# One DMA transpose per attention weight tile instead of two to four, a fourth running-product buffer, and the carries on VectorE

## The chip, the cores and the metric

The kernel runs on one NeuronCore of a Trainium2 chip. The metric is the time of one execution on the device, in microseconds (us). The median over several runs is what is compared.

The core has five engines that each work through their own list of instructions in order: TensorE (PE, with its weight loads PEld), VectorE (DVE), ScalarE (ACT), GpSimd (POOL) and SyncE (SP), which here issues nearly all DMA transfers. Waits between engines go by semaphores. The order on each engine was fixed when the program was built.

## The reference

One layer of a decoder block over 1024 positions of width 1024. It has a mixer (stick-breaking attention with 8 heads of 64, and a short gated convolution, both gated and added) and a convolutional feed-forward part. The change touches the attention weights alone:

```python
for blk in range(s // Q_BLOCK):            # 128 queries at a time
    z = einsum("bhqd,bhkd->bhqk", qb, kb) * scale
    log_keep = where(strict, log_sigmoid(-z), 0)
    later = cumsum(log_keep, reverse=True) - log_keep
    w = where(strict, exp(log_sigmoid(z) + later), 0)
    o = einsum("bhqk,bhkd->bhqd", w, vb)
```

So each weight is sigmoid(z) times the product of sigmoid(-z) over all later keys.

## The kernel before

Every large product is made from float16 high and low halves of its operands, in three passes (high by high, high by low, low by high). The program is laid out by a scheduler that was given priorities, which writes one fixed order for each engine.

The mixer runs attention and projections at the same time. The projections (q, k and the three convolution inputs of head pair j+1, values, branches) are fill work on TensorE between the steps of attention. There are four head pairs j (two heads each, called h); a pair takes about 79 us of the trace. A pair has six units: unit j_p_b is the query blocks 2p and 2p+1 against up to 512 keys from key block b on. A unit has two half tiles, tl = 1 and tl = 0, one for each query block, so there are 4 x 6 x 2 = 48 half tiles. W, the number of keys of a half tile, is 128 to 512; a half tile has 2W columns, since it holds both heads. `stage1` makes a half tile:

- TensorE computes z into one of two PSUM buffers (line 451; 455 adds the mask).
- ScalarE writes sigmoid(-z) to the tile R (line 464) and sigmoid(z) to be (line 465). R has three buffers, and its last column W holds the start of the running product: GpSimd sets it to a constant (line 461) or copies it from the unit with later keys (463).
- VectorE turns R into a running product from the right (468, one scan for each head). GpSimd saves column 0 as the carry for the next unit (472).
- VectorE multiplies be by the product (473), ScalarE writes the high half of the weights over R (476), and VectorE the low half (477).
- SP turns the halves by DMA transposes into the tile wT (483). R is free again when the last of them has landed.

`stage3` multiplies values by wT (line 505) two units later; TensorE waits there for the transposes, and line 514 empties the result. wT has five buffers, each for one half (high or low) of one unit.

The high and the low half are turned apart. When a half tile is narrower than its unit's tl = 1 tile (always so for tl = 0 of units at the diagonal), the two heads are turned apart as well, so it takes four transposes instead of two. That makes 128 transposes. A transpose of 2W columns moves 2W/128 blocks of 128 x 128.

Of the kernel before, what the change touches and what calls it, by code (L numbers as in the profile page):

```python
# [16 lines left out]
F16 = mybir.dt.float16  # L17
BF16 = mybir.dt.bfloat16
F32 = mybir.dt.float32
# [5 lines left out]
P = 128  # L25
# [3 lines left out]
NH = 512  # L29
# [8 lines left out]
class Layer:  # L38
# [232 lines left out]
    def mixer(self, mid):  # L271
        tc, nc, a = self.tc, self.nc, self.a
        hT = self.hp.tile([P, 2, KD, T], F16, tag="hT", name="hT")
        with ExitStack() as ph1:
# [166 lines left out]
            def stage1(u, tt, tl):  # L441

                j, i, lo, nm = u["j"], tt, u["lo"], f"{u['nm']}{tl}"
                s = stk[j]
                W = min(NH, (i + 1) * P - lo)
                nb = W // P
                z = pat.tile([P, 2, NH], F32, tag="z", name=f"z{nm}", bufs=2)
                for n, (hq, hk) in enumerate(PASSES):
                    for h in range(2):
                        d = ds(64 * h, 64)  # L450
                        m = nc.tensor.matmul(z[:, h, :W], s["q"][d, hq, ds(i * P, P)], s["k"][d, hk, ds(lo, W)],
                                             start=n == 0, stop=n == 2 and not u["top"], skip_group_check=True)
                if u["top"]:
                    for h in range(2):
                        m = nc.tensor.matmul(z[:, h, W - P:W], self.identb, self.maskb, start=False, stop=True,
                                             skip_group_check=True)
                u["last"] = m
                R = att.tile([P, 2, NH + 1], F32, tag="R", name=f"R{nm}", bufs=3)
                be = att.tile([P, 2, NH], F32, tag="be", name=f"be{nm}", bufs=2)
                if u["top"]:  # L460
                    nc.gpsimd.memset(R[:, :, W:W + 1], 2.0 ** 14)
                else:
                    nc.gpsimd.tensor_copy(R[:, :, W:W + 1], carry[tl])
                nc.scalar.activation(R[:, :, :W], z[:, :, :W], AF.Sigmoid, scale=s["cz"][1])  # L464
                nc.scalar.activation(be[:, :, :W], z[:, :, :W], AF.Sigmoid, scale=s["cz"][0])
                for h in range(2):
                    rev = R[:, h, 0:W][:, ::-1]
                    nc.vector.tensor_tensor_scan(rev, rev, self.zero.broadcast_to([P, W]),  # L468
                                                 2.0 ** 14 if u["top"] else carry[tl][:, h, :], ALU.mult, ALU.add)
                if not u["end"]:  # L470
                    carry[tl] = self.smp.tile([P, 2, 1], F32, tag="cy", name=f"cy{nm}", bufs=4)
                    nc.gpsimd.tensor_copy(carry[tl], R[:, :, 0:1])
                nc.vector.tensor_tensor(be[:, :, :W], be[:, :, :W], R[:, :, 1:W + 1], ALU.mult)  # L473
                w = R.rearrange("p h s -> p (h s)").bitcast(F16)[:, :4 * NH].rearrange("p (l x) -> p l x", l=2)
                wv = [w[:, hl, :2 * W].rearrange("p (h s) -> p h s", h=2) for hl in range(2)]
                nc.scalar.activation(wv[0], be[:, :, :W], AF.Copy)  # L476
                nc.vector.tensor_tensor(wv[1], be[:, :, :W], wv[0], ALU.subtract)  # L477
                NB = u["nb"]
                for hl in range(2):
                    for h in ((None,) if nb == NB else range(2)):  # L480
                        src = w[:, hl, :2 * W] if h is None else w[:, hl, ds(h * W, W)]
                        dst = u["wT"][hl][:, ds(0 if h is None else h * NB, 2 * nb if h is None else nb), tl, :]
                        nc.sync.dma_start_transpose(dst, src)

            carry = {}
            acc = {}
# [1 line left out]
            def stage3(u, after):  # L488
# [7 lines left out]
                with tc.issue_after(after):  # L496
                    for q, (hw, hv) in enumerate(((1, 0), (0, 0), (0, 1))):
                        for b in range(NB):
                            sb = lo // P + b
                            both = sb <= 2 * p  # L500
                            for h in range(2):
                                rhs = u["wT"][hw][:, h * NB + b, :, :] if both else u["wT"][hw][:, h * NB + b, 1, :]
                                out = o[64 * h:64 * h + 64, n0:n0 + 2 * P] if both else \
                                    o[64 * h:64 * h + 64, n0 + P:n0 + 2 * P]
                                nc.tensor.matmul(out, v16[sb // 2][:, sb % 2, j, 1 + h if hv else 3 * h, :], rhs,  # L505
                                                 start=first and q == 0 and b == 0, stop=q == 2 and b == NB - 1,
                                                 skip_group_check=True)
# [11 lines left out]
            def attention():  # L519
                us = list(units_of())  # L520
                lag = 2
                for k in range(len(us) + lag):
                    if k < len(us):
                        u = us[k]
                        while "cz" not in stk.get(u["j"], {}):
                            yield 0
                        u["wT"] = [att.tile([P, 8, 2, P], F16, tag="wT", name=f"wT{u['nm']}_{hl}", bufs=5) for hl in range(2)]
                        for tl in (1, 0):
                            with tc.high_priority():
                                stage1(u, 2 * u["p"] + tl, tl)  # L530
# [604 lines left out]
```

## Time and profile before

| | |
|---|---|
| median of 3 runs | 1377.57 us (1376.06 to 1377.88) |
| the profiled execution | 1375.74 us |
| its span, first instruction to last | 1374.0 us |
| TensorE busy | 1303.2 us (95%) |
| VectorE busy | 1002.5 us (73%) |
| ScalarE busy | 804.2 us (59%) |
| GpSimd busy | 73.9 us (5%) |
| transposes, first and last start | 75.9 us and 365.0 us |
| share of the granted TensorE clock | 0.988 |

Busy time counts an engine's own instructions. The chain of waits says for each idle stretch what ended it. Idle time of an engine costs nothing unless TensorE, which is nearly always busy, waits for it in the end.

### The profile page before, as it was taken

To read this page: it belongs to the slowest core of one execution; us is meant where nothing else is said; L and a number is where in the kernel's file an instruction comes from. 1 tells how busy PE (TensorE), PEld (TensorE's weight loads), DVE (VectorE), ACT (ScalarE), POOL (GpSimd) and SP (SyncE) were. 2 spreads that over 40 slices of the span, in tenths; PEclk is the share of its full clock that TensorE was granted. 3 is DMA by queue.
4 is the path that set the end of the run, shared out by engine and by line. 5 is a ranking of instruction groups with operands and counts; after the bars stand their busy time and mean duration, and the time that the engine had idled before them with its cause. 6 is when DMAs were issued, how large, how long until landed. Compare 5 with 4: busy or idle time off the path is not lost. (4 is left out here: it accounts for less than half of the span.)

```text
span 1374.0 us, 17361 instructions
## 1 busy us (share of the span) xinstructions
PE 1303.2 (95%) x6543; PEld 600.8 (44%) x6543; DVE 1002.5 (73%) x1585; ACT 804.2 (59%) x1138; POOL 73.9 (5%) x133
## 2 busy tenths in 40 slices
PE   5998899898989999999999999999999999999997
PEld 3444344343434444444444444444444444444443
DVE  5669696867642997877788867954982893698857
ACT  6656665556455465665555676764754764566422
POOL 1001010100000000000110000010001001000001
PEclk9999999999999999999999999999999999999999
DMA  7235344434411011241331134256227318713115
GB/s 262 77 66 109 76 105 92 98 81 102 104 42 51 16 62 60 75 172 62 123 123 47 47 141 166 62 125 152 62 92 137 117 56 203 221 49 108 62 73 188
DMA packets 111957, 139.63 MB, mean 102 GB/s; under 512 B 81648, under 2 KB 81648, under 8 KB 111872
## 3 DMA queue, kind: packets, MB, share of 16 engines
q1 hardware_dynamic: 107920, 124.29, 30.2%
q0 software_dynamic: 3952, 14.23, 5.6%
q8 instruction: 51, 0.84, 0.3%
q14 instruction: 34, 0.28, 0.1%
HBM read 94.45 MB, written 25.17 MB: 87 GB/s over the span
## 5 line engine op out<-in xcount | busy, mean ns | idle before, releaser
L1005 PEld LDWEIGHTS <-wh_u 128*128 128x128 f16 x1848 | 178.8, 98 | 217.8 <-issue 4.0
L900 PE MATMUL pd<-wdh,f 128*128 128x512 f16 x1056 | 232.2, 381 | 10.2 <-DVE wdh L87 5.7
L900 PEld LDWEIGHTS <-f 128*128 128x128 f16 x1056 | 103.6, 98 | 137.3 <-issue 12.1
L1005 PEld LDWEIGHTS <-wh_g 128*128 128x128 f16 x588 | 56.8, 98 | 70.7 <-ACT wh_g L86 2.3
L715 PE MATMUL py<-wh_wo,m 128*128 128x512 f16 x384 | 83.9, 379 | 0.0
L76 DVE TENSOR_SCALAR sc<-pr 128x1 int32<-128x1 int32 x75 | 10.7, 150 | 94.8 <-PE pr L74 94.6
L464 ACT ACTIVATE R<-z,cz 128x1024 f32<-128x1024 f32 (+3 forms) x48 | 42.7, 897 | 62.1 <-DMA wT<-R 41.9
L87 DVE SCALAR_TENSOR_TENSOR wh_u<-ws_u,sc,wh_u 128x1024 f16<-128x1024 f32 (+1 forms) x66 | 72.1, 1100 | 8.9 <-ACT wh_u L86 8.9
L86 ACT ACTIVATE wh_u<-ws_u,sc 128x1024 f16<-128x1024 f32 (+1 forms) x66 | 64.2, 998 | 22.5 <-DVE ws_u L840 12.6
L904 ACT ACTIVATE y<-pd,sd 128x512 f32<-128x512 f32 x64 | 42.1, 693 | 57.7 <-PE pd L900 51.3
L1082 DVE SCALAR_TENSOR_TENSOR ugu<-cgu,cw_g,ugu 128x1023 f32<-128x1023 f32 (+1 forms) x44 | 56.2, 1278 | 9.9 <-ACT ugu L1080 9.7
L468 DVE TENSOR_TENSOR_SCAN R<-R,zero 128x256 f32<-128x256 f32 (+3 forms) x64 | 48.7, 807 | 17.6 <-ACT R L464 17.5
L1082 DVE SCALAR_TENSOR_TENSOR ua<-cau,cw_a,ua 128x1023 f32<-128x1023 f32 (+1 forms) x44 | 56.2, 1277 | 2.0 <-ACT ua L1080 1.8
L715 PEld LDWEIGHTS <-m 128*128 128x128 f16 x384 | 37.5, 98 | 44.0
L476 ACT ACTIVATE R<-be 128x1024 f16<-128x1024 f32 (+3 forms) x48 | 39.9, 841 | 24.5 <-DVE be L473 17.6
L468 DVE TENSOR_TENSOR_SCAN R<-R,cy,zero 128x512 f32<-128x512 f32 x32 | 39.3, 1269 | 16.1 <-ACT R L464 16.0
L477 DVE TENSOR_TENSOR R<-be,R 128x1024 f16<-128x1024 f32 (+3 forms) x48 | 45.1, 948 | 8.0 <-ACT R L476 8.0
L505 PE MATMUL o<-wT,v 128*64 128x256 f16 (+1 forms) x480 | 41.6, 295 | 8.6 <-DVE o L514 5.7
L56 ACT ACTIVATE jk_u<-ws_u 128x1024 bf16<-128x1024 f32 x44 | 46.4, 1055 | 2.7 <-DMA ws_u<-w_up_nt 2.0
L203 PE MATMUL pcc<-hT,wh_cc 128*128 128x512 f16 x192 | 45.1, 389 | 3.0 <-DVE pf L394 3.0
L307 PE MATMUL pv<-wh_v,hT 128*128 128x512 f16 x192 | 45.2, 391 | 2.7 <-ACT wh_v L86 1.9
L473 DVE TENSOR_TENSOR be<-be,R 128x1024 f32<-128x1024 f32 (+3 forms) x48 | 45.5, 951 | 2.2
(606 smaller groups left out, 2572.6 us busy)
## 6 DMA issues: line engine op xcount, KB each, us to landing
ws_u<-w_up_nt SPq DMA_DIRECT2D x44, 512.0 KB, 3.5
yd<-y POOLq DMA_DIRECT2D x24, 512.0 KB, 5.2
ds<-w_down SPq DMA_DIRECT2D x22, 512.0 KB, 6.6
wd<-w_down SPq DMA_DIRECT2D x22, 512.0 KB, 3.6
ws_g<-w_in_nt SPq DMA_DIRECT2D x14, 512.0 KB, 3.5
x<-x SPq DMA_DIRECT2D x8, 512.0 KB, 9.0
ws_wo<-w_out SPq DMA_DIRECT2D x8, 512.0 KB, 6.7
xr<-x SPq DMA_DIRECT2D x8, 512.0 KB, 4.0
```

What stands on the lines that cost most here:

```text
L56: self.nc.scalar.activation(self.junk(f"jk_{name}"), src, AF.Square, accum_out=acc)
L86: self.nc.scalar.activation(dst[:, 0, :], src, AF.Copy, scale=s)
L87: self.nc.vector.scalar_tensor_tensor(dst[:, 1, :], src, s, dst[:, 0, :], ALU.mult, ALU.subtract)
L203: nc.tensor.matmul(ps, w[:, wi, ds(k * P, P)], hT[:, hi, k, ds(c * NH, NH)], start=n == 0, stop=n == last)
L307: nc.tensor.matmul(pv, hT[:, hi, k, ds(tt * P, P)], wv[k // 2][:, wi, ds((k % 2) * NH, NH)], start=n == 0, stop=n == 3 * KD - 1)
L468: nc.vector.tensor_tensor_scan(rev, rev, self.zero.broadcast_to([P, W]), 2.0 ** 14 if u["top"] else carry[tl][:, h, :], ALU.mult, ALU.add)
L473: nc.vector.tensor_tensor(be[:, :, :W], be[:, :, :W], R[:, :, 1:W + 1], ALU.mult)
L477: nc.vector.tensor_tensor(wv[1], be[:, :, :W], wv[0], ALU.subtract)
L715: nc.tensor.matmul(ps, m16[k][:, hi, ds(tt * P, P)], wo[k][:, wi, sl], start=k == 0 and p == 0, stop=k == 7 and p == 2)
L900: nc.tensor.matmul(ps, f16[g][k][:, hi, ds(tt * P, P)], w[k][:, wi, sl], start=n == 0, stop=n == 3 * GROUPS[g] - 1)
L1005: nc.tensor.matmul(ps, w[wt][:, wi, ds(wc * NH + k * P, P)], self.block(i, hi, k), start=first and n == 0, stop=n == 3 * KH - 1, skip_grou ...
L1082: nc.vector.scalar_tensor_tensor(u[:, lag:], c[:, :T - lag], sm[:, 2 - lag:3 - lag], u[:, lag:], ALU.mult, ALU.add)
```

## The change

Three edits in `stage1`, and what follows from them in `stage3` and where wT is made:

- The high half is now packed into the first 2W columns of the 16-bit view of R and the low half into the next 2W, so that one transpose of 4W columns turns both halves of both heads. wT is one tile per unit with two buffers, laid out half tile by half tile; `stage3` picks its blocks by a step. There are 48 transposes, of 4, 8, 12 or 16 blocks.
- R has four buffers instead of three.
- The constant or carry at column W, and the saved carry, are written by VectorE: 32 memsets, 16 copies into R and 16 copies out of it.

```diff
-                R = att.tile([P, 2, NH + 1], F32, tag="R", name=f"R{nm}", bufs=3)
+                R = att.tile([P, 2, NH + 1], F32, tag="R", name=f"R{nm}", bufs=4)
...
-                    nc.gpsimd.memset(R[:, :, W:W + 1], 2.0 ** 14)
+                    nc.vector.memset(R[:, :, W:W + 1], 2.0 ** 14)
                 else:
-                    nc.gpsimd.tensor_copy(R[:, :, W:W + 1], carry[tl])
+                    nc.vector.tensor_copy(R[:, :, W:W + 1], carry[tl])
...
-                    nc.gpsimd.tensor_copy(carry[tl], R[:, :, 0:1])
+                    nc.vector.tensor_copy(carry[tl], R[:, :, 0:1])
...
-                w = R.rearrange("p h s -> p (h s)").bitcast(F16)[:, :4 * NH].rearrange("p (l x) -> p l x", l=2)
-                wv = [w[:, hl, :2 * W].rearrange("p (h s) -> p h s", h=2) for hl in range(2)]
+                w = R.rearrange("p h s -> p (h s)").bitcast(F16)[:, :4 * W]
+                wv = [w[:, ds(2 * W * hl, 2 * W)].rearrange("p (h s) -> p h s", h=2) for hl in range(2)]
...
-                NB = u["nb"]
-                for hl in range(2):
-                    for h in ((None,) if nb == NB else range(2)):
-                        src = w[:, hl, :2 * W] if h is None else w[:, hl, ds(h * W, W)]
-                        dst = u["wT"][hl][:, ds(0 if h is None else h * NB, 2 * nb if h is None else nb), tl, :]
-                        nc.sync.dma_start_transpose(dst, src)
+                nc.sync.dma_start_transpose(u["wT"][:, ds(tl * 4 * u["nb"], 4 * nb), :], w)
...
-                                rhs = u["wT"][hw][:, h * NB + b, :, :] if both else u["wT"][hw][:, h * NB + b, 1, :]
+                                k0, k1 = (2 * hw + h) * nb0 + b, (2 * hw + h) * NB + b + 4 * NB
+                                rhs = u["wT"][:, k0:k1 + 1:k1 - k0, :] if both else u["wT"][:, k1, :]
...
-                        u["wT"] = [att.tile([P, 8, 2, P], F16, tag="wT", name=f"wT{u['nm']}_{hl}", bufs=5) for hl in range(2)]
+                        u["wT"] = att.tile([P, 32, P], F16, tag="wT", name=f"wT{u['nm']}", bufs=2)
```

The scheduler writes a new order. On SP, in the second head pair, this is the stretch of units 1_1 and 1_2_4 before (names are R and wT with pair, unit and half tile; 128x8x128 is eight blocks, and x2 is two in a row):

```order
L483 DMA_TRANSPOSE wT1_1_0_0_1475<-R1_1_01_1486 128x8x128
L483 DMA_TRANSPOSE wT1_1_0_1_1476<-R1_1_01_1486 128x8x128
L483 DMA_TRANSPOSE wT1_1_0_0_1475<-R1_1_00_1551 128x3x128 x2
L483 DMA_TRANSPOSE wT1_1_0_1_1476<-R1_1_00_1551 128x3x128
L483 DMA_TRANSPOSE wT1_2_4_0_1650<-R1_2_41_1661 128x4x128
L483 DMA_TRANSPOSE wT1_2_4_0_1650<-R1_2_40_1693 128x1x128 x2
L483 DMA_TRANSPOSE wT1_2_4_1_1651<-R1_2_41_1661 128x4x128
L483 DMA_TRANSPOSE wT1_1_0_1_1476<-R1_1_00_1551 128x3x128
L483 DMA_TRANSPOSE wT1_2_4_1_1651<-R1_2_40_1693 128x1x128 x2
L103 DMA ws_k3_0_1635<-w_in_nt 128x1024
```

And the same stretch of SP in the changed kernel:

```order
L478 DMA_TRANSPOSE wT1_1_0_1444<-R1_1_01_1454 128x16x128
L478 DMA_TRANSPOSE wT1_1_0_1444<-R1_1_00_1518 128x12x128
L478 DMA_TRANSPOSE wT1_2_4_1614<-R1_2_41_1624 128x8x128
L478 DMA_TRANSPOSE wT1_2_4_1614<-R1_2_40_1655 128x4x128
L103 DMA ws_k3_0_1599<-w_in_nt 128x1024
```

Twelve transposes have become four, ahead of the same weight load.

On VectorE, where the second pair goes from unit 1_0 to unit 1_1, the rows before are these (468 is the scan, 473 and 477 the products, 87 a weight split, 514 empties a stage 3 result):

```order
L477 TENSOR_TENSOR R1_0_01_1384<-be1_0_01_1385,R1_0_01_1384 128x512
L477 TENSOR_TENSOR R1_0_00_1419<-be1_0_00_1420,R1_0_00_1419 128x256
L90 TENSOR_TENSOR cz2_1920<-sc8_1089,sc9_1204 128x1
L90 TENSOR_TENSOR cz2_1920<-cz2_1920,cst_438 128x1 x2
L87 SCALAR_TENSOR_TENSOR wh_k2_0_1212<-ws_k2_0_959,sc9_1204,wh_k2_0_1212 128x1024
L468 SCALAR_TENSOR_TENSOR R1_1_01_1486<-R1_1_01_1486,zero_102 128x512 x2
L473 TENSOR_TENSOR be1_1_01_1487<-be1_1_01_1487,R1_1_01_1486 128x1024
L468 SCALAR_TENSOR_TENSOR R1_1_00_1551<-R1_1_00_1551,zero_102 128x384 x2
L514 SCALAR_TENSOR_TENSOR o16_0_1041<-o0_2_4_1174,o16_0_1041 128x512
```

In the changed kernel the same place on VectorE reads:

```order
L477 TENSOR_TENSOR R1_0_01_1357<-be1_0_01_1358,R1_0_01_1357 128x512
L477 TENSOR_TENSOR R1_0_00_1391<-be1_0_00_1392,R1_0_00_1391 128x256
L90 TENSOR_TENSOR cz2_1874<-sc8_1069,sc9_1181 128x1
L90 TENSOR_TENSOR cz2_1874<-cz2_1874,cst_438 128x1 x2
L87 SCALAR_TENSOR_TENSOR wh_k2_0_1189<-ws_k2_0_942,sc9_1181,wh_k2_0_1189 128x1024
L461 MEMSET R1_2_41_1624 128x2
L461 MEMSET R1_2_40_1655 128x2
L468 SCALAR_TENSOR_TENSOR R1_1_01_1454<-R1_1_01_1454,zero_102 128x512 x2
L468 SCALAR_TENSOR_TENSOR R1_1_00_1518<-R1_1_00_1518,zero_102 128x384 x2
```

Two memsets of unit 1_2_4's R now stand ahead of the scans of unit 1_1. With four buffers they write the two that unit 1_0 used, whose last VectorE writes are the two rows on top.

## Rows read from the trace of the kernel before

**Rows 1.** The page: its head and TensorE's busy time.

```profile
span 1374.0 us, 17361 instructions
...
PE 1303.2 (95%) x6543; PEld 600.8 (44%) x6543; DVE 1002.5 (73%) x1585; ACT 804.2 (59%) x1138; POOL 73.9 (5%) x133
```

**Rows 2.** Windows: attention; stretch, busy PE, PEld, DVE, ACT, POOL, clock, DMA, GB/s.

```profile
60.00:375.00 315.00, 290.66 (x1795) 135.98 (x1794) 235.27 (x355) 184.88 (x247) 26.59 (x61) 0.96 0.43 94
```

**Rows 3.** Waits of PE, 60 to 390 us: total us, times, longest.

```profile
PE z L451 <- ACT be L465: 7.4, 9, 2.7
PE o L505 <- DVE o L514: 5.7, 5, 1.6
PE pcc L203 <- DVE pf L394: 3.0, 1, 3.0
PE o L505 <- DMA wT<-R: 2.8, 7, 0.6
PE pk L203 <- DVE q L360: 2.2, 2, 1.1
PE pcb L203 <- DVE u L392: 2.0, 3, 0.8
```

**Rows 4.** Waits of ACT and DVE, 60 to 390 us.

```profile
ACT R L464 <- DMA wT<-R: 41.9, 14, 5.6
...
ACT R L476 <- POOL cy L472: 5.8, 4, 1.8
...
DVE R L468 <- ACT R L464: 33.5, 16, 5.6
```

**Rows 5.** Timeline near 153 and 250 us: start, us, instruction, [idle before <- releaser].

```profile
153.05 0.50 PE L451 MATMUL z<-k,q 64*128 64x128 f16 x6 [2.75 <-ACT be L465]
...
247.92 1.12 ACT L464 ACTIVATE R<-z,cz 128x1024 f32<-128x1024 f32 x1 [5.63 <-DMA wT<-R]
...
249.06 2.46 DVE L468 TENSOR_TENSOR_SCAN R<-R,cy,zero 128x512 f32<-128x512 f32 x2 [4.03 <-ACT R L464]
...
250.09 0.82 PE L451 MATMUL z<-k,q 64*128 64x512 f16 x6 [0.57 <-ACT be L465]
```

**Rows 6.** Timeline of SP in two stretches: start, us, instructions.

```profile
86.17 16.55 SPq L483 DMA_TRANSPOSE wT<-R  x12
...
235.62 14.82 SPq L483 DMA_TRANSPOSE wT<-R  x11
```

**Rows 7.** Line 483: issue ns; us to landing: two one-block transposes, then three eight-block ones.

```profile
L483 SPq DMA_TRANSPOSE wT<-R x2: 1183/1204/1224, 100.3 to 101.5; - x2
...
DMA to landing us min/median/max: 2.3/2.3/2.3
...
L483 SPq DMA_TRANSPOSE wT<-R x3: 1245/1257/1288, 106.3 to 112.2; - x3
...
DMA to landing us min/median/max: 3.1/3.2/3.2
```

**Rows 8.** Windows: first two of four attention stretches at clock 0.50, and their sum.

```profile
118.20:121.60 3.40, 2.84 (x30) 2.00 (x26) 3.40 (x6) 3.29 (x6) 1.06 (x2) 0.50 0.35 71
152.30:159.10 6.80, 5.36 (x29) 2.61 (x29) 5.38 (x8) 5.52 (x9) 0.10 (x1) 0.50 0.64 155
...
sum 23.80, PE 21.80 PEld 11.47 DVE 22.38 ACT 15.37 POOL 5.79; mean PE 5.45 PEld 2.87 DVE 5.59 ACT 3.84 POOL 1.45
```

**Rows 9.** DVE instructions by shape: busy us, mean ns; the first line min/median/max ns.

```profile
L252 DVE MEMSET one<- x1: 59/59/59, 1.0 to 1.0; 128x1 f32 x1
...
L102 DVE COPY ws_wo<-ywa 128x1 f32<-128x1 f32 x8 | 0.7, 143 | 0.0
...
L90 DVE TENSOR_TENSOR cz<-cz,cst 128x1 f32<-128x1 f32 x8 | 0.9, 155 | 0.1
...
L477 DVE TENSOR_TENSOR R<-be,R 128x256 f16<-128x256 f32 x8 | 3.3, 418 | 0.0
...
L87 DVE SCALAR_TENSOR_TENSOR wh_k<-ws_k,sc,wh_k 128x1024 f16<-128x1024 f32 x4 | 5.1, 1279 | 0.2 <-ACT wh_k L86 0.2
```

More of the change, by code (lines that the diff above doesn't have):

```diff
@@ L500, in stage3 @@
                             both = sb <= 2 * p
+                            nb0 = min(NB, 2 * p + 1 - lo // P)
                             for h in range(2):
-                                rhs = u["wT"][hw][:, h * NB + b, :, :] if both else u["wT"][hw][:, h * NB + b, 1, :]
+                                k0, k1 = (2 * hw + h) * nb0 + b, (2 * hw + h) * NB + b + 4 * NB
+                                rhs = u["wT"][:, k0:k1 + 1:k1 - k0, :] if both else u["wT"][:, k1, :]
                                 out = o[64 * h:64 * h + 64, n0:n0 + 2 * P] if both else \
```

## Prediction

> **What bounds the kernel now.** I began with the page. TensorE is busy for 1303.2 of 1374.0 us [rows 1], so a change that leaves its matmuls alone, as this one does, can only win back idle time and slow clock. The change touches 75.9 to 365 us, so I read the windows next. Between 60 and 375 us TensorE is busy for 290.66 of 315 us, VectorE for 235.27 and ScalarE for 184.88 [rows 2]. That leaves 24.3 us of TensorE's idle time, and VectorE is idle for 79.7 us.
>
> TensorE's own waits split those 24 us [rows 3]. Two kinds belong to the path that is changed. For 7.4 us it waits at z until ScalarE has read a z buffer, and for 2.8 us at line 505 for a transpose. The other four rows, 12.9 us, are VectorE's lateness: it empties a PSUM bank late (514, 394, 360, 392).
>
> Then I asked why ScalarE reads z late. It waits 41.9 us for transposes to free R, and VectorE waits 33.5 us for ScalarE in turn [rows 4]. One instance shows the whole chain. At 247.92 ScalarE had waited 5.63 us for a transpose before it could write R; VectorE's scan at 249.06 came after 4.03 us of idling; TensorE's z came 0.57 us late [rows 5]. The reader should see that the loss shrinks on its way: 5.6 us on ScalarE is 0.57 us on TensorE at that z, since fill work lies in between.
>
> The transposes are late there because of SP. It issues eleven or twelve in a row, 16.55 us for 12 and 14.82 us for 11 [rows 6]. One block takes 1.20 us to issue and eight take 1.26; they land 2.3 and 3.1 to 3.2 us after the issue starts [rows 7]. So the issue is paid per transpose and hardly per block, and R waits in a queue on SP.
>
> Last, the clock. Four attention stretches, 23.80 us with TensorE busy for 21.80, ran at a granted clock of 0.50, the 1.2 GHz level [rows 8]. Work in them takes twice as long, so they cost some 10.9 us.
>
> **The change, part by part.** *One transpose.* SP issues 48 instead of 128. At 1.3 us each (an estimate for 16 blocks: eight cost 0.06 us more than one, so sixteen some 0.1 us more) that is 62 us instead of about 160. The burst of twelve becomes four, 5 us instead of 16.55. A single large tile gains nothing: from one to eight blocks the landing grows by 0.85 us, 0.12 a block, which puts sixteen at 4.1 us (estimate). Bounds are 3.15, no slower than eight, and 5.05, its part after the issue doubled. Before, the second of two eight-block transposes could start right after line 477 and land after 3.15. So R of a full tile comes free about 1 us later than before when SP is idle, and much earlier when SP is full. The Trainium skill's "DMA: Bandwidth & Descriptors", section "Latency and other measured facts", gives 261 GB/s for a transpose with a non-contiguous middle dimension and 350 to 400 for a contiguous one. The old destination skipped every second block and the new one is contiguous. Rows 7 give 7 blocks of 32 KB in 0.85 us, about 270 GB/s, which agrees with the first figure; by the second, sixteen blocks would land at some 3.6 us (estimate from that page), which would take 0.75 us off the 3.0 us of the new wait below.
>
> *Fourth buffer.* With three buffers a half tile takes over the R of the third one before it, now of the fourth: the old owner is done one half tile sooner. With the shorter burst I expect nearly all of ScalarE's 41.9 us to go. On TensorE this is worth at most 7.4 + 2.8 us; I take 5.5 and 2.0, three quarters, because ScalarE and VectorE also queue behind one another in the pair's busy end. The bounds are 0 and 10.2.
>
> *Clock.* The slow stretch from 152.30 to 159.10 [rows 8] opens inside a wait at z for ScalarE, which ended at 153.05 after 2.75 us [rows 5]. If that wait goes I expect the stretch to go: half of its 5.36 busy us, 2.7. The one from 118.20 has 2.84 busy us and several small waits around it; I count half of its 1.4. Together 3.4 us; the other two I leave. Bounds 0 and 10.9.
>
> *Carries on VectorE.* It gains 64 instructions. A memset of one column took it 59 ns and a one-column copy 143 ns [rows 9]: 32 x 0.059 + 32 x 0.143 = 6.5 us. It has 79.7 idle us in the stretch, which hides most, but not at the end of each pair, where it works without a break; there the memsets and copies delay the emptying that TensorE waits for. I take 1.7 us, a quarter; bounds 0 and 6.5. GpSimd's copies, for which ScalarE waited 5.8 us [rows 4], go; that helps the chain and is inside the three quarters above.
>
> *A new wait on VectorE.* The memset and the copy into R must wait until the transpose of R's last owner has landed. GpSimd could wait there without harm; behind VectorE's wait stand scans, weight splits and PSUM evictions. In the new order I added up what stands between line 477 of the old owner and the new first write. For R1_2_41, shown above: 0.42 + 3 x 0.155 + 1.28 = 2.2 us [rows 9] against a landing of 3.15, so it stands for 1.0, and its neighbour, one issue later, for 0.45 more. Unit 3_4 has the same pattern, about 1.6. At the start of the next pair two memsets follow two 16-block transposes with 2.0 us between, so some 2.1. That is about 5 us for a pair, and 19 for four with three such starts. All other first writes have 4.4 us or more of work ahead of them. The first two places stand right before scans, at which VectorE idled 33.5 us anyway, so I count them as covered. The third stands before evictions of q and k: half of 3 x 2.1, 3.0 us. Bounds 0 and 19.
>
> *wT in two buffers* instead of five halves costs nothing: stage 3 of unit k-2 stands behind z of unit k on TensorE, and unit k's transposes come only after two scans and two products of VectorE. If that cover went, SP would stand, with weight loads behind it. The strided pick of blocks in line 505 leaves each run of 128 columns whole, so I cost it at nothing.
>
> Sum: -5.5 - 2.0 - 3.4 + 1.7 + 3.0 = -6.2 us. The profiled execution, 1375.74 us (its span and 1.7 us around it), becomes 1369.5. It was 1.83 us under the median of the runs, which becomes **1371.4 us**.
>
> **Rivals.** *More than the direct waits.* If VectorE is late only because it idled 4 us in each pair for R, then its 12.9 us on TensorE and the rest of the slow clock (7.5 us) shrink too. All of it would give 1371.4 - 20.4 = 1351; half gives 1361. For it: 33.5 us of idling on an engine whose lateness costs 12.9. Against it: the evictions come at the end of a pair, where VectorE is dense.
>
> *VectorE takes it back.* Removing 4 us of idling a pair and adding 1.6 us of work and some 3 of the new waits leaves VectorE where it was; TensorE's 7.5 us come back as later evictions, and the clock stays. The time is 1377, within 0.2%.
>
> *The new wait decides: slower.* If all 19 us of standing and all 6.5 us of work lie on TensorE's path, against 10.9 us of gains, the time is 1377.6 + 14.6 = 1392; with half of the standing and the work, 1379. It is slower than before once more than 10.9 of those 25.5 us reach TensorE. For it: VectorE is 75% busy in the stretch, and everything queues behind its wait. Against it: two of three places come before scans.
>
> *The issue grows with size.* If 16 blocks took two eight-block issues, 2.5 us, the bursts would shrink only by the transposes cut in two by head, and R of a full tile would come later; the fourth buffer would win a part: about 1375. From one to eight blocks the issue grew by 0.05 us only, so this is unlikely. The Trainium skill has it: "DMA: Bandwidth & Descriptors", under "Why a DMA increments its semaphore by 16 and not by 1", lists for earlier generations 262,144 sequencer cycles for 8,192 tiles of such a transpose, a cost for each tile; rows 7 do not show one.
>
> **How the numbers follow.** A measurement of this kernel tells about 0.2% from no change, 2.8 us. The forecast (1363 to 1374.8) gets 0.47, more than that 0.17, VectorE taking it back 0.17, the growing issue 0.04, and slower 0.15. Faster is then 0.64, same 0.21, slower 0.15. The range 1358 to 1381 leaves out the larger half of the first rival and the worse half of the slow one, about 2 in 10. Given a gain, I expect 1358 to 1374.8.
>
> **What would show it.** Right: 48 transposes of about 1.3 us, landing in 2.4 to 4.3; ScalarE's waits for wT under 10 us; TensorE's wait at z under 2.5 us; VectorE's waits for a transpose at lines 461 and 463 below 20 us in all, with evictions no later. Wrong: a VectorE wait for transposes above 20 us while TensorE's waits for evictions (12.9 us now) grow; landing above 5 us; an issue above 2 us; or new slow-clock stretches.

## The result, and the profile after

The changed kernel takes **1386.05 us** (median of 4 runs, 1384.96 to 1389.26), the kernel before 1377.72 beside it: a ratio of 1.0065 [1.0046, 1.0085]. It is slower by about 9 us, where the prediction had 1371.4 and a gain.

The page of the profiled execution (1389.26 us): head and busy times.

```profile
span 1387.5 us, 17025 instructions
...
PE 1299.4 (94%) x6543; PEld 598.0 (43%) x6543; DVE 1004.6 (72%) x1649; ACT 804.7 (58%) x1138; POOL 48.2 (3%) x69
```

VectorE has gained 2.1 us of busy time [rows 1] and TensorE has lost 3.8, so no engine simply has more to do. The loss is over early: the first matmul of the branches (line 422) starts at 405.8 us instead of 394.1, and from there on the two spans differ by 2 us only (981.7 and 979.9). The window of attention:

```profile
60.00:375.00 315.00, 273.88 (x1732) 127.41 (x1731) 235.38 (x409) 181.94 (x242) 0.00 (x0) 0.93 0.44 93
```

TensorE is busy for 16.8 us less than before in the same stretch, at a lower clock, 0.93 for 0.96 [rows 2]. Not all of this is idling: z and o themselves take TensorE less time now (fourth round). From 60 us to the first matmul of the branches it idles 45.2 us of 345.8, against 28.4 of 334.1 before. Waits of TensorE, VectorE and ScalarE between 60 and 390 us (in all, times, longest):

```profile
PE o L502 <- DVE o L511: 12.7, 5, 4.2
PE o L502 <- DMA wT<-R: 12.3, 7, 5.0
PE pq L203 <- DVE pf L394: 11.0, 2, 5.5
PE pk L203 <- DVE R L461: 4.3, 1, 4.3
PE z L451 <- ACT be L465: 0.4, 2, 0.2
```

```profile
DVE R L461 <- DMA wT<-R: 16.4, 13, 3.2
...
DVE R L468 <- ACT R L464: 10.8, 4, 3.8
...
DVE R L463 <- DMA wT<-R: 5.2, 8, 1.2
```

```profile
ACT R L476 <- DVE be L473: 39.4, 20, 4.4
ACT be L465 <- DVE R L477: 14.5, 13, 4.0
```

What was to go did go: the wait at z fell from 7.4 to 0.4 us [rows 3], ScalarE no longer waits for a transpose at all (41.9 before), and VectorE's scans wait 10.8 us for ScalarE instead of 33.5 [rows 4]. In its place VectorE stands for 21.6 us (16.4 + 5.2) at its small writes into R, ScalarE waits for VectorE (39.4 and 14.5 us, 17.6 and 4.3 before), and TensorE waits for evictions: 12.7 us at line 511 (5.7 before at 514) and 11.0 at 394 (3.0 before). Two more waits for transposes, 2.8 and 2.2 us, are the memsets' as well: the view puts them down to a row of another line that starts with the memset. With them VectorE stands for 26.6 us.

Two places show the two mechanisms. The first is VectorE's timeline at the place in the second pair whose order stands ahead of the prediction, the memsets of unit 1_2_4's R before the scans of unit 1_1, and TensorE's timeline behind it:

```profile
152.80 0.06 DVE L461 MEMSET R<- 128x2 f32 x1 [3.24 <-DMA wT<-R]
153.20 1.22 DVE L468 TENSOR_TENSOR_SCAN R<-R,zero 128x512 f32<-128x512 f32 x1 [0.33 <-issue]
...
157.15 2.07 DVE L473 TENSOR_TENSOR be<-be,R 128x1024 f32<-128x1024 f32 x2
...
159.20 0.68 DVE L511 SCALAR_TENSOR_TENSOR o<-o,o 128x512 f16<-128x512 f32 x1
```

```profile
159.93 1.17 PE L502 MATMUL o<-wT,v 128*64 128x256 f16 x12 [4.24 <-DVE o L511]
```

A write of 0.06 us stood 3.24 us for a transpose. Scans, products and the eviction at line 511 came that much later, and TensorE idled 4.24 us for the eviction. A half-clock stretch opened in this gap.

The second place, 120 us later:

```profile
277.55 1.22 DVE L473 TENSOR_TENSOR be<-be,R 128x1024 f32<-128x1024 f32 x1
277.57 0.06 DVE L461 MEMSET R<- 128x2 f32 x1
278.68 2.46 DVE L468 TENSOR_TENSOR_SCAN R<-R,cy,zero 128x512 f32<-128x512 f32 x2
281.05 0.73 DVE L394 SCALAR_TENSOR_TENSOR pf<-pcb,cv,pf 128x512 f32<-128x512 f32 x1
```

```profile
281.84 1.44 PE L203 MATMUL pq<-hT,wh_q 128*128 128x512 f16 x3 [5.51 <-DVE pf L394]
```

Here VectorE doesn't wait. It works without a break, but the eviction at 394 stands behind the two scans of the pair's last half tile (2.46 us). In the kernel before, the eviction stood ahead of these scans in all of the pairs 2 to 4, here in the same pair:

```profile
275.22 0.74 DVE L394 SCALAR_TENSOR_TENSOR pf<-pcb,cv,pf 128x512 f32<-128x512 f32 x1
275.88 1.22 DVE L473 TENSOR_TENSOR be<-be,R 128x1024 f32<-128x1024 f32 x1
277.20 2.46 DVE L468 TENSOR_TENSOR_SCAN R<-R,cy,zero 128x512 f32<-128x512 f32 x2
```

In the changed kernel the scheduler put it behind in all three.

The slow clock grew with the gaps: eight half-clock stretches between 60 and 411 us sum to 47.60 us (before, the four of [rows 8] and a fifth of 3.4 us from 394.7 on, 27.2 us in all), and every one holds a gap of TensorE or follows one; the two at the places above:

```profile
158.10:164.90 6.80, 4.97 (x23) 2.21 (x23) 6.71 (x15) 4.92 (x8) 0.00 (x0) 0.50 0.43 80
...
280.90:287.70 6.80, 5.86 (x14) 2.08 (x14) 5.87 (x13) 3.56 (x5) 0.00 (x0) 0.50 0.41 78
```

The transposes (issue in ns, then the time to landing, each least, median and most):

```profile
L478 SPq DMA_TRANSPOSE wT<-R x48: 1209/1470/3013, 79.7 to 370.3; - x48
...
DMA to landing us min/median/max: 2.5/4.3/5.9
```

### The profile page after: what moved, and what is told of

The parts are those of the page before. It is cut to its first block, busy times and chain, and to the rows that moved or that the text cites. A ratio compares the mean times of both kernels' runs of the same rounds, so it can differ in the third digit from the quotient of the medians.

```text
span 1387.5 us, 17025 instructions
## 1 busy us (share of the span) xinstructions
PE 1299.4 (94%) x6543; PEld 598.0 (43%) x6543; DVE 1004.6 (72%) x1649; ACT 804.7 (58%) x1138; POOL 48.2 (3%) x69
## 5 line engine op out<-in xcount | busy, mean ns | idle before, releaser
L76 DVE TENSOR_SCALAR sc<-pr 128x1 int32<-128x1 int32 x75 | 10.8, 152 | 110.0 <-PE pr L74 109.9
L86 ACT ACTIVATE wh_u<-ws_u,sc 128x1024 f16<-128x1024 f32 (+1 forms) x66 | 64.2, 998 | 22.6 <-DVE ws_u L837 12.6
L476 ACT ACTIVATE R<-be 128x1024 f16<-128x1024 f32 (+3 forms) x48 | 39.2, 839 | 51.3 <-DVE be L473 39.4
L203 PE MATMUL pq<-hT,wh_q 128*128 128x512 f16 x192 | 50.3, 422 | 13.1 <-DVE pf L394 11.0
L468 DVE TENSOR_TENSOR_SCAN R<-R,zero 128x256 f32<-128x256 f32 (+3 forms) x64 | 47.9, 804 | 16.1 <-ACT R L464 10.8
L465 ACT ACTIVATE be<-z,cz 128x1024 f32<-128x1024 f32 (+3 forms) x48 | 42.4, 903 | 23.0 <-DVE R L477 14.5
L502 PE MATMUL o<-wT,v 128*64 128x256 f16 x480 | 31.0, 281 | 25.2 <-DVE o L511 12.7
L203 PE MATMUL pk<-hT,wh_k 128*128 128x512 f16 x192 | 45.5, 395 | 4.6 <-DVE R L461 4.3
L203 PE MATMUL pcx<-hT,wh_cx 128*128 128x512 f16 x192 | 46.0, 388 | 0.0
```

Of the source, the lines that this page charges most:

```text
L86: self.nc.scalar.activation(dst[:, 0, :], src, AF.Copy, scale=s)
L203: nc.tensor.matmul(ps, w[:, wi, ds(k * P, P)], hT[:, hi, k, ds(c * NH, NH)], start=n == 0, stop=n == last)
```

## The experiments

Ratios are to the kernel before, run beside each kernel. All experiments compute the whole reference.

### First round: which edit costs?

Three theories. **Standing:** VectorE's waits for transposes at lines 461 and 463 hold up all that is queued behind them. **Landing:** the large transposes land later, and all that needs them is late. **Order:** the scheduler's new order puts evictions behind scans, whoever waits.

*x1.* ScalarE instead of VectorE writes column W, from a constant tile or the carry.

```diff
-                    nc.vector.memset(R[:, :, W:W + 1], 2.0 ** 14)
+                    nc.scalar.activation(R[:, :, W:W + 1], self.seed, AF.Copy)
...
-                    nc.vector.tensor_copy(R[:, :, W:W + 1], carry[tl])
+                    nc.scalar.activation(R[:, :, W:W + 1], carry[tl], AF.Copy)
```

> The changed kernel, but ScalarE instead of VectorE writes the constant or carry into column W of R, directly ahead of its own write of R (which waits for the same landing); VectorE only saves the carry. TensorE's and VectorE's order are nearly those of the changed kernel. Three theories. Standing (VectorE stands at lines 461 and 463 until R's last transpose has landed, 16.4 + 5.2 us in the trace, and the evictions behind it are late): most of the loss goes, 1372 to 1378 us, and TensorE's waits for line 511 and 394 fall from 23.7 us to about 12. Landing (the large transposes land 4.3 instead of 3.1 us after their issue, and the high half no longer goes ahead): stays at 1383 to 1387. Order (the new order itself puts evictions behind scans and products on VectorE, and TensorE runs ahead of it): stays at 1383 to 1387.

Measured 1392.54 us, 1.0098 [1.0077, 1.0119]: slower still. ScalarE now stands for transposes, 41 us in all, and VectorE's scans wait 36.6 us for it. The run moved the wait rather than removing it, so it doesn't decide between Standing and Order, and it missed the ranges of all three theories.

*x2.* All three small operations back on GpSimd; merge and four buffers stay.

```diff
-                    nc.vector.memset(R[:, :, W:W + 1], 2.0 ** 14)
+                    nc.gpsimd.memset(R[:, :, W:W + 1], 2.0 ** 14)
...
-                    nc.vector.tensor_copy(R[:, :, W:W + 1], carry[tl])
+                    nc.gpsimd.tensor_copy(R[:, :, W:W + 1], carry[tl])
...
-                    nc.vector.tensor_copy(carry[tl], R[:, :, 0:1])
+                    nc.gpsimd.tensor_copy(carry[tl], R[:, :, 0:1])
```

> The changed kernel with all three small operations on GpSimd, as before (merged transposes and four buffers stay). Standing: 1369 to 1376 us, what was forecast without the new wait. Landing: 1382 to 1387. Order: the ScalarE order is that of the changed kernel, VectorE's is partly that of before, so 1378 to 1386.

Measured **1356.87 us**, 0.9844 [0.9816, 0.9871], faster than both kernels. Its transposes are as large as the changed kernel's and land as late (median 4.3 us in both), so Landing falls. The time is below all three ranges, Standing's too by 12 us. The view of the transposes' line says who waits now:

```profile
  POOL R L461: 147.0, 26
  POOL R L463: 16.0, 11
```

GpSimd stands for 163 us for the same transposes. Its list there holds hardly anything but these small operations, 60 instructions from 60 to 375 us.

*x3 and x4.* Three buffers instead of four, in the changed kernel (x3) and with GpSimd's operations as in x2 (x4: the merge alone).

```diff
-                R = att.tile([P, 2, NH + 1], F32, tag="R", name=f"R{nm}", bufs=4)
+                R = att.tile([P, 2, NH + 1], F32, tag="R", name=f"R{nm}", bufs=3)
```

> The changed kernel with three R buffers instead of four. Standing: each first write waits for a tile that was finished one half tile later, so VectorE stands far longer, over 40 us, and the time is 1395 us or more. Landing: 1390 to 1395, since the later landing is waited for more often. Order: between 1378 and 1390, as the order happens to fall.

> Only the merged transposes (wT in two buffers); three R buffers, small operations on GpSimd. Standing: VectorE does not stand, SP's bursts are shorter: 1372 to 1378 us. Landing: R of a full tile comes free 1 us later and its three buffers are the bottleneck: 1382 to 1390. Order: 1376 to 1386.

x3 measured 1375.38 us, 0.9981 [0.9964, 0.9998]; x4 1365.42, 0.9904 [0.9882, 0.9926]. Both are faster than every range that was given for them. The expectation that fewer buffers make the standing worse was wrong: VectorE stands 15.3 us in x3 (10.7 + 4.6, lines 461 and 463) against 21.6. The carries on VectorE cost 10 us with three buffers (x3 against x4) and 29 with four (the change against x2).

### Second round: the wait, the work or the order

*y4.* No column W. The last column of be is multiplied by the start factor in an operation of its own, so VectorE keeps its 64 small operations and its order, and none of them waits for a transpose.

```diff
-                if u["top"]:
-                    nc.vector.memset(R[:, :, W:W + 1], 2.0 ** 14)
...
+                if u["top"]:
+                    nc.vector.tensor_scalar(be[:, :, W - 1:W], be[:, :, W - 1:W], 2.0 ** 14, None, ALU.mult)
+                else:
+                    nc.vector.tensor_tensor(be[:, :, W - 1:W], be[:, :, W - 1:W], carry[tl], ALU.mult)
...
-                nc.vector.tensor_tensor(be[:, :, :W], be[:, :, :W], R[:, :, 1:W + 1], ALU.mult)
+                nc.vector.tensor_tensor(be[:, :, :W - 1], be[:, :, :W - 1], R[:, :, 1:W], ALU.mult)
```

> The changed kernel without column W: VectorE multiplies the last column of be by the start factor (the constant, or the saved carry) in an operation of its own, and line 473 multiplies the other W - 1 columns by R shifted by one. VectorE has as many small operations as in the changed kernel, but none of them writes R before ScalarE has, so none waits for a transpose. TensorE's and ScalarE's orders stay as in the changed kernel (4 and 0 rows differ), VectorE's too but for the small operations. Standing (the wait for the transpose at lines 461 and 463, with everything behind it on VectorE, costs the time): 1355 to 1368 us, and the waits of TensorE for lines 511 and 394 fall from 23.7 to under 12 us. Order (the order that the scheduler made costs it, whoever waits): 1382 to 1390 us, and those waits stay above 18 us. Work (the small operations themselves cost it): 1382 to 1390 us as well, since their number stays.

Measured 1368.72 us, 0.9922 [0.9909, 0.9935], 0.7 us above Standing's range and far below the others': the standing costs 0.0143, 20 us. But TensorE's waits for 511 and 394 fell only to 14.4 us, not under 12:

```profile
PE o L502 <- DMA wT<-R: 11.3, 7, 5.1
PE pq L203 <- DVE pf L394: 11.1, 2, 5.6
...
PE o L502 <- DVE o L511: 3.3, 1, 3.3
```

The wait at 511 is mostly gone and 394 isn't touched. So there are two mechanisms.

*y3.* Lines 461 and 463 stand behind the two activations in the text, and so some rows later in VectorE's list.

> The changed kernel with lines 461 and 463 moved behind the two activations in the text, which moves the small writes some rows down VectorE's list and leaves every other order as it is. VectorE still waits for the transpose there, but later, when more of the landing is over. Standing: in between, 1362 to 1380 us, with VectorE's waits for wT at these writes falling from 21.6 to under 14 us. Order and Work: 1383 to 1389 us.

Measured 1380.40 us, 0.9999 [0.9988, 1.0011], 0.4 us above Standing's range. VectorE's waits at the small writes fell from 21.6 to 9.3 us in the trace of this run: the later the write stands, the less it holds up. Standing's number for the wait (under 14) is met, its time just missed.

*y1 and y2.* The three small operations split: in y1 GpSimd writes column W and VectorE saves the carry; in y2 the other way round (lines as in x2).

> The changed kernel with the writes to column W (461, 463) back on GpSimd and the saved carry (472) on VectorE. No VectorE operation waits for a transpose at the writes. Standing: 1355 to 1365 us, since 472 waits for VectorE's own scan alone. Work: 16 copies of 32 + 32 operations stay, 1360 to 1372 us. Order (TensorE's order differs from the changed kernel's by 84 rows and from that with all three on GpSimd by more): above 1370 us.

> The changed kernel with the saved carry (472) on GpSimd and the writes (461, 463) on VectorE. Standing: the wait stays, and a carry made by GpSimd later adds to it; 1383 to 1395 us. Work: the 16 copies that leave give back little, 1380 to 1386 us. If the saves were the cost, 1357 to 1368 us.

y1 measured 1368.39 us, 0.9929 [0.9910, 0.9947]: like y4, the standing is gone. The time lies in Work's range (1360 to 1372), above Standing's; the third round tells the two apart (z2). It is some 12 us slower than x2, from which only the 16 saved carries differ, and its order shows where: in x2 the eviction at 394 stands ahead of the scans of R_3_00 in pairs 2 to 4, in y1 behind them. y2 measured 1381.26 us, 1.0020 [1.0007, 1.0032], 6 us faster than the changed kernel and just below Standing's range, in Work's; one of the three evictions stands ahead there.

### Third round: the evictions alone

Theory **Eviction:** these three swaps cost their 2.65 us each on TensorE, doubled where a half-clock stretch follows. One edge holds the scans of a pair's last half tile behind the eviction, in four kernels: the changed one (z1), y1 (z2), y4 (z3) and x4 (z4). Lines move down by up to 7 in these kernels: 397 is 394, 518 is 511.

```diff
+                            if c == 0:
+                                cb0.append(ev.ins)
...
+                held = cb0[j - 1:j] if j and (u["p"], lo, tl) == (3, 0, 0) else []
...
+                    with tc.issue_after(held[0]) if held else nullcontext():
+                        nc.vector.tensor_tensor_scan(rev, rev, self.zero.broadcast_to([P, W]),
```

> The changed kernel with one thing held in VectorE's list: in pairs 2 to 4 the eviction at line 394 stands ahead of the scans of the last half tile (R_3_00), as it does in the kernel before, and not behind them (8 of VectorE's rows differ, 50 of TensorE's, none of ScalarE's). The scans take 2.65 us. Eviction (these three swaps cost their 2.65 us each, and the slow clock that follows a wait of 5.5 us): 1386 less 8 to 12, 1373 to 1379 us, and TensorE's waits for line 394 fall from 5.5 to about 2.8 us each. Standing alone (the waits for the transposes at 461 and 463 are the whole cost): 1383 to 1388 us.

> Column W written by GpSimd, the carry saved by VectorE (1368.4 us), with the evictions at line 394 held ahead of the scans of the last half tile. Eviction: the whole distance to the kernel with all three operations on GpSimd (1356.9 us) goes, 1355 to 1360 us. If the 16 copies on VectorE themselves cost the time: 1366 to 1370 us.

> No column W (1368.7 us), all small operations on VectorE, with the evictions at line 394 held ahead of the scans of the last half tile. Standing and Eviction together are then both gone from the changed kernel with no operation moved back to GpSimd: 1355 to 1361 us. If work on VectorE matters for itself: 1364 to 1370 us.

> One transpose, three buffers for R, GpSimd's carries (1365.4 us), with the evictions at line 394 held ahead of the scans of the last half tile. There the scans stood first as well, and with four buffers (1356.9 us) the evictions did. If the fourth buffer's gain of 8.5 us is only this swap: 1355 to 1359 us. If the buffer itself gives it: 1362 to 1367 us, with ScalarE's 29 us of waits for R unchanged.

z1 1377.81 us, 0.9985 [0.9969, 1.0001]; z2 **1356.73**, 0.9832 [0.9813, 0.9850]; z3 1358.84, 0.9847 [0.9828, 0.9866]; z4 1366.95, 0.9907 [0.9887, 0.9926]. Eviction's times held in z1, z2 and z3; z4 stayed where the buffer itself was to give the gain. In z1 the wait that was 5.51 us reads:

```profile
274.17 2.30 PE L204 MATMUL pq<-hT,wh_q 128*128 128x512 f16 x8 [3.16 <-DVE pf L397]
```

With merge and four buffers the ratios make a table, in which each mechanism has its own price whatever the other does:

| | evictions first | evictions behind the scans |
|---|---|---|
| VectorE doesn't stand | 0.9844 (x2), 0.9832 (z2), 0.9847 (z3) | 0.9922 (y4), 0.9929 (y1) |
| VectorE stands | 0.9985 (z1) | 1.0065 (the change) |

Standing costs 0.0136 to 0.0153, 19 to 21 us; the evictions 0.0075 to 0.0097, 10 to 13 us. z3 has all small operations on VectorE and is as fast as x2 with all on GpSimd: as work they cost nothing that can be measured (the intervals are some 2.7 us to either side). In z4 the swap changes nothing, so x4's distance to x2 isn't made by it.

The same runs place the wait for transposes at line 502, which had grown from 2.8 to 12.3 us. It is 11.3 to 12.6 us with the evictions behind the scans (the change, y1, y3, y4) and 5.4 to 6.9 with them first (x2, z1, z2, z3), with transposes of the same sizes. So its larger part goes with the evictions' place, not with the size of the transposes.

### Fourth round: where the gain came from

x2 wins 21.5 us, twice the 10.9 that the prediction counted. The trace of before offers a cause that it had not looked at, TensorE's order (the granted clock here is 0.99):

```profile
184.27 0.30 PE L505 MATMUL o<-wT,v 128*64 128x256 f16 x1 [1.13 <-DVE o L514]
184.50 0.39 PE L451 MATMUL z<-k,q 64*128 64x512 f16 x1
184.81 0.30 PE L505 MATMUL o<-wT,v 128*64 128x256 f16 x1
185.04 0.39 PE L451 MATMUL z<-k,q 64*128 64x512 f16 x1
```

An o takes 0.23 us from its start to the next, a z 0.31. In the changed kernel 24 o in a row take 1.50 us, 0.06 each, at a granted clock of 1.00; the two heads run side by side, their starts 3 to 5 ns apart:

```profile
147.76 1.50 PE L502 MATMUL o<-wT,v 128*64 128x256 f16 x24
```

From start to start, all z and o together take 75.0 us before and 54.1 in x2 (each matmul counted up to 0.7 us, those of the mask left out). Theory **Pairs**: this is the gain. Theory **Waits**: it comes from the waits for R.

*w1 and w2.* The z matmuls are held behind the stage 3 ahead of them, in the kernel before (w1) and in x4 (w2). *w3.* The kernel before with four buffers for R alone, and four halves of wT.

```diff
+                with tc.issue_after(o_end[0]) if o_end else nullcontext():
+                    for n, (hq, hk) in enumerate(PASSES):
```

> The kernel before, with the z matmuls of a half tile held behind the last o matmul of the stage 3 ahead of them in the program, so that TensorE works off runs of o and of z instead of one o, one z, one o, one z (33 single o matmuls become 4, 24 single z matmuls none). In the trace before an o alone takes 229 ns and a z alone 316 ns from its start to the next, while within a run two o of both heads take 109 ns together and two z 216. Pairs (a good part of what the merge and the fourth buffer won is that TensorE's order lets the two heads run side by side again): 1362 to 1371 us, with the time from starts to starts of all z and o falling from 75 to under 62 us. Waits (it is won from waits for R and for SP alone): 1375 to 1382 us, since R is as late as before.

> One transpose, three buffers for R, carries on GpSimd (1365.4 us), with the z matmuls held behind the stage 3 ahead of them as in the run above. With four buffers the scheduler makes unbroken runs by itself. Pairs: most of the fourth buffer's 8.5 us comes without the buffer, 1355 to 1360 us. Waits: 1364 to 1370 us, with ScalarE's 29 us of waits for R as long or longer.

> The kernel before with a fourth buffer for R alone (and four halves of wT instead of five, for the space); 128 transposes, carries on GpSimd. 28 single o matmuls and 10 single z stay, so the order is broken nearly as often as before. Pairs: little is won, 1372 to 1380 us. Waits: the fourth buffer takes away the waits for R that the long bursts of SP cause, 1362 to 1371 us.

w1 measured 1381.13 us, 1.0005 [0.9993, 1.0017]; w2 1373.98, 0.9960 [0.9945, 0.9975]; w3 1375.71, 0.9969 [0.9959, 0.9980]. Alone, Pairs falls: in w1 z and o take 12 us less (63.1), and the time stays. TensorE waits instead, 11.7 us at z (7.4 before) and more for evictions:

```profile
PE z L453 <- ACT be L467: 11.7, 7, 3.3
PE o L508 <- DVE o L518: 7.3, 5, 1.9
PE pq L204 <- DVE pf L395: 5.4, 2, 4.1
PE pcc L204 <- DVE pf L395: 5.0, 1, 5.0
```

So with R as late as before, TensorE isn't what ends last there. That the chain through R is, is argued from its waits. w2 missed both ranges; w3 lies in the range of Pairs and missed that of Waits; and in w2 and w3 the evictions had slipped behind the scans.

*v1 and v2.* w3 and w2 with the evictions held first, as in z1. *v3.* x2 with the high and the low half turned by a transpose each, both heads together: 96 transposes.

```diff
-                nc.sync.dma_start_transpose(u["wT"][:, ds(tl * 4 * u["nb"], 4 * nb), :], w)
+                for hl in range(2):
+                    nc.sync.dma_start_transpose(u["wT"][:, ds(tl * 4 * u["nb"] + 2 * nb * hl, 2 * nb), :], w[:, ds(2 * W * hl, 2 * W)])
```

> The kernel before with a fourth buffer for R (1375.7 us), with the evictions at line 394 held ahead of the scans of the last half tile; there the scheduler had put them behind, and TensorE waits 6.0, 5.3 and 2.6 us for them. Eviction: 8 to 12 us come back, 1363 to 1368 us. If the evictions behind the scans cost only together with VectorE's carries: 1372 to 1377 us.

> One transpose, three buffers, GpSimd's carries, z held behind stage 3 (1374.0 us), with the evictions at line 394 held ahead of the scans of the last half tile. TensorE waits 4.2 and 4.3 us for them there. Eviction: 1364 to 1369 us. If the unbroken order pays once the evictions are early (TensorE's time in z and o is 13 us shorter than in the merge alone): 1355 to 1361 us.

> The changed kernel with GpSimd's carries (1356.9 us), but the high and the low half turned by a transpose each, both heads together: 96 transposes of 2 to 8 blocks instead of 48 of 4 to 16; R with four buffers, orders of TensorE and VectorE nearly the same (12 and 8 rows). If turning the halves together is what pays (half of the issues on SP): 1362 to 1370 us. If it is enough that the heads are turned together: 1355 to 1360 us. If the 16-block transposes land too late (4.3 us): under 1355 us.

v1 measured 1362.30 us, 0.9888 [0.9867, 0.9910], 0.7 us below Eviction's range; v2 1364.15, 0.9899 [0.9878, 0.9920]; v3 1356.75, 0.9846 [0.9823, 0.9870]. The fourth buffer alone, with the evictions first, wins 15 us. v2 equals x4, so with three buffers unbroken runs win nothing even then. v3 equals x2: it is enough that both heads are turned together; joining the halves, the edit that gives the change its name, adds nothing. Its transposes are shorter and land earlier; that this makes up for their number isn't shown:

```profile
L479 SPq DMA_TRANSPOSE wT<-R x96: 1178/1232/2397, 77.3 to 344.3; - x96
...
DMA to landing us min/median/max: 2.3/3.1/4.8
```

What Pairs leaves open shows in TensorE's time from 60 us to its first matmul of the branches, in before, x2 and w1 (stretch, then TensorE's busy time):

```profile
60.00:394.10 334.10, 305.72 (x1865) 142.77 (x1864) 243.52 (x380) 190.42 (x255) 26.59 (x61) 0.96 0.42 92
...
60.00:374.50 314.50, 288.38 (x1867) 135.16 (x1866) 242.61 (x380) 189.77 (x255) 21.90 (x60) 0.98 0.44 97
...
60.00:397.60 337.60, 295.87 (x1863) 140.57 (x1862) 244.62 (x379) 190.82 (x255) 26.07 (x61) 0.96 0.42 91
```

Of the 19.6 us that x2 wins here, 17.3 are busy time of TensorE and 2.3 idle time. In w1 the busy time falls by 9.9 us and the idle time grows by 13.4. So most of x2's gain is shorter work on TensorE, as Pairs says (z and o above all, and less of it at the half clock). That it is kept only where R comes early enough, as Waits says, fits w1 and is argued. No run has merge and four buffers with the order broken as before, so what each gives by itself isn't separated.

## Why the prediction was wrong

By the runs the sum is -21.5 (merge and fourth buffer, x2) + 19 (standing, z1 against z3) + 11 (evictions, the change against z1, by the ratios), +8.5 us; measured were about 9. The sum closes because z3 equals x2; the independent check is the table, where each price comes out alike in both rows and columns.

**The step that failed is "A new wait on VectorE".** The wait was foreseen and its sum came near: 19 us of standing were estimated from the order, 21.6 came (26.6 with the two waits that stand under other lines). Its price was taken as 3.0 of 19 and is 19 to 21. The error stands in one sentence: the first two places "stand right before scans, at which VectorE idled 33.5 us anyway, so I count them as covered". By the estimate these two take 12.2 us in the four pairs; they took 19.7 (unit 2_4 11.2, unit 3_4 8.5). The start of the next pair, the only place with a price, was to take 6.3 us and took none. The first writes that were to have "4.4 us or more of work ahead of them" took 6.9. So nearly three quarters of the standing lay where it had been counted as free. The start of the second pair, and then the two places in the fourth:

```profile
129.89 0.06 DVE L461 MEMSET R<- 128x2 f32 x1
...
314.47 0.06 DVE L461 MEMSET R<- 128x2 f32 x1 [1.55 <-DMA wT<-R]
316.75 1.22 DVE L468 TENSOR_TENSOR_SCAN R<-R,zero 128x512 f32<-128x512 f32 x1 [2.23 <-DMA wT<-R]
316.75 0.06 DVE L461 MEMSET R<- 128x2 f32 x1
...
333.27 0.06 DVE L461 MEMSET R<- 128x2 f32 x1 [1.00 <-DMA wT<-R]
335.55 0.06 DVE L461 MEMSET R<- 128x2 f32 x1 [2.22 <-DMA wT<-R]
```

The 33.5 us that were to cover it were VectorE's wait for ScalarE, which waited for R, and the same change took most of that wait away: 12.6 us are left with the merge alone (x4), 23.4 with the buffer alone (w3), 11.4 with both (x2):

```profile
DVE R L468 <- ACT R L464: 12.6, 14, 3.2
...
DVE R L468 <- ACT R L464: 23.4, 13, 3.8
...
DVE R L468 <- ACT R L464: 11.4, 11, 3.1
```

So one edit's cover was what the other edits removed. That it would have covered the wait without them is argued: no run puts the carries on VectorE in the kernel before. At 152.80 the wait stands right before scans, 3.24 us for the estimated 1.0 (the transpose issued at 147.76 landed after 5.0 us, not 3.15), and TensorE idles 4.24 us behind it. The rival "the new wait decides" had the mechanism and the sign, with 0.15.

**A step was missing.** That the scheduler would turn round the eviction at 394 and the scans of the last half tile in three pairs (11 us) was in no term. It can be read from the order before any run: both orders are fixed. The prediction looked at the order only where the new instructions stand, not at the rows that TensorE waited for (394 stands in [rows 3]).

**Merge and fourth buffer: direction right, size half.** 7.5 us of waits and 3.4 of clock were counted, 21.5 came, the size that the rival "more than the direct waits" had. But the working began with the premise that a change which leaves TensorE's matmuls alone "can only win back idle time and slow clock", and that failed: in x2 idle time gave 2.3 of 19.6 us, and z and o, the same matmuls in another order, became 20.9 us shorter (what the half clock gave back there included). That the size fits the rival is partly luck. With the evictions first the merge wins 13 alone (z4), the buffer 15 (v1), both 21.5. ScalarE's waits for transposes, 41.9 us before, are 24.7, 13.0 and none there; that both edits take away the same waits, so that the second finds less, fits this and is argued. The slow clock fell as well: x2 has one half-clock stretch of 6.8 us and three of 3.4 between 60 and 411 us, 17.0 against 27.2 before.

**Carries as work:** 1.7 us taken; z3 against x2 shows none, but 1.7 us would be lost in the intervals. A memset took 60 ns, a copy 0.14 to 0.17 us, near [rows 9].

**One transpose:** a landing of 4.1 us was estimated for 16 blocks; the 24 of them in the changed kernel had a median of 4.32, and the eight with 8 blocks 3.21 (landings sorted by size). That is 8 x 32 KB more in 1.11 us, about 236 GB/s. The Trainium skill's "DMA: Bandwidth & Descriptors", section "Latency and other measured facts", gives some 350 to 400 GB/s for the contiguous case; this trace doesn't agree: the rate is below even the 261 that it gives for a non-contiguous one. The issue was taken as 1.3 us and has a median of 1.90 at 16 blocks (least 1.32, most 3.01; 1.23 at eight): as near to the rival of a growing issue (2.5) as to the forecast. It did no harm that shows: v3, with 96 issues for 48, is as fast as x2.

**wT in two buffers** and the strided pick: x2 and z3 show no cost that stands out; they weren't tried by themselves.

Of the list of what would show it, "evictions' waits grow" and "new slow-clock stretches" came true, beside a standing above 20 us; a landing above 5 us and an issue above 2 us came only singly (2 and 5 of 48).

What stays open, beside the split of the gain: why x1 is slower than the changed kernel itself, since the standing there moved to ScalarE and the evictions stood behind the scans as well; and why the standing costs some 19 us with four buffers but 10 with three (x3 against x4); the shorter waits there, 15.3 us for 21.6, go the same way, but no run separates them.

## What to carry to other kernels

Before a wait is called covered, ask whether the idle time that covers it is what the same change removes. An instruction that must wait for a buffer's release belongs on an engine with nothing behind it, however slow that engine is (163 us of standing on GpSimd were free, 21.6 on VectorE cost some 20), or is best done without (z3). A new order can also make the same matmuls take less time, as z and o did. Compare the order not only where instructions come and go but at each row that the critical engine waited for: a swap of an eviction with 2.5 us of scans, three times, was worth 11 us, and one edge put it right.

## What the runs showed of the hardware that wasn't expected

- Two matmuls of 64 columns (line 505), or two of 64 rows (line 451), overlap when they follow one another: 24 o take 1.50 us, 62 ns each, and the two heads' o start 3 to 5 ns apart; six z of 512 columns take 0.82 us [rows 5]. Where o and z alternate, an o takes 0.23 us and a z 0.31. The Trainium skill's "TensorE: Matmul & The Clock Gate", "Part 3: Packing small matmuls — row/col tiling", has matmuls at different tile positions start some 4 ns apart; the runs of one kind agree. That alternating kinds lose the overlap is shown by this trace.
- The issue of a transpose grows between 8 and 16 blocks, from a median of 1.23 to 1.90 us, after hardly any growth from 1 to 8, 1.20 to 1.26 [rows 7]. Four of the 24 with 16 blocks took under 1.4 us, so the size alone doesn't set it.
